# Seven-product MLP, first product: sums formed in seeded PSUM banks, and some deferred steps deferred further

## The chip, the cores and the metric

The kernel runs on one core of one Trainium2 chip. A core has TensorE (PE, matrix products; a weight load, PEld, precedes each and overlaps the one before), VectorE (DVE), ScalarE (ACT), GpSimd (POOL) and SyncE (SP, which issues most transfers). Each engine works off its own instructions in order and waits on semaphores for the others. The metric is the time of one execution on the device in microseconds (us); lower is better.

## The reference, cut to what matters

One encoder layer for 2048 tokens of width 1024: a mixer (attention in two head groups), then an MLP. The change lies in the MLP, mostly in its first product `h @ w1`.

```python
x = x + gt1 * (mixed @ w_o[l])
h = rmsnorm(x, g_norm2[l]) * (1.0 + sc2) + sh2
x = x + gt2 * (jnp.square(jax.nn.relu(h @ w1[l])) @ w2[l])
```

`w1` is 1024 x 4096, `w2` 4096 x 1024, all float32.

## The kernel before

**Tiling.** Everything is stored transposed: features on the partitions, tokens along the row. After the mixer and its output projection (class `Mixed`, eight steps), the MLP is one list `steps` that a loop at the end of the program walks through. The tokens are cut in two halves, `mb` = 1 and then 0, each half into two blocks of 512.

**Seven products.** A 2 x 2 block product is made with seven block products in place of eight (Strassen in Winograd's form). In class `First`, a group `j` (16 per half) is 256 rows of hidden units: two row blocks by two token blocks, contracted over 1024 features in two halves. Sums of the weights' four blocks come from POOL (`sums`, four operations, tiles `ts` and `w`); the sums of the activations' blocks were made ahead (`right_blocks`, tiles `h`). Each of the seven products, named 1 to 7 here as in the code, is one step: four contraction blocks, and for each three matmuls (`mm3`), because every float32 operand is split into a high and a low float32r part. So a step is 12 matmuls of 128 x 512, a group is 84, a half is 1344. Operands are prepared seven or eight steps ahead: ACT casts the high part and DVE subtracts to get the low part (tile `opw`).

**How the products are summed before.** They run in the order 1, 6, 5, 7, 2, 3, 4. Products 1, 6, 5, 7 and 3 each open a bank of PSUM; 2 goes on in the bank of 1, and 4 in that of 7. The other sums are made by DVE on the way out of PSUM: with u = 1 + 6 and v = u + 5, the four results are c11 = 1 + 2, c12 = v + 3, c22 = v + 7 and c21 = u + (7 + 4). ACT copies 1 into SBUF (tile `cu`); DVE adds 6 to it (`cu`), 5 (`cv`), 7 (`cx`), 3 (`cv`) and 4 (`cu`). ACT then applies ReLU and the square to each result (`hidden`, in SBUF; for c11, tile `cy`, straight from PSUM). DVE makes three differences and one more (`ca`, `cb`, `cv`, `ce`) that the second MLP product needs, and SP stores the seven tiles (`keep`, to `scr_hid`).

**Other work in the same steps.** In half 1, `second_sums` (DVE, tile `w2s`) and in half 0 `outer_sums` (DVE, tile `wt`) form sums of `w2` blocks, at the third to sixth step of nearly every group, and SP stores them. `norm2` gets the norm of a token block: ACT squares and DVE sums eight tiles, then `second` sends the sum through PE (`pvm`), POOL and DVE (`ndgm`), and `third` spreads it with PE (`psr`). The second MLP product follows in classes `Second` and `Outer`; `Outer` already works in the order 1, 5, 6, 3, 7, 2, 4 with seeded banks (`ps_s`), and `update` adds results to rows of x and stores them.

**What sets the order.** Program order is the order of the loop: at each step the operands of a later step are prepared, then jobs registered for this step run (`at`), then the step's matmuls and what follows them (`run`), then `later.tick()`, which runs whatever `later.add(n, ...)` put off by n ticks. The loads of `w1` (`load`, tile `w`) stand in SP's queue at the second step of the group two before the one that uses them, behind all the stores of the group before. Banks come from eight buffers in three groups (`zb` four, `ab` two, `db` two); an object of `Banks` hands them out in rotation, `pp` from all three.

Of the kernel before, what the change touches and what calls it, by code (L numbers as in the profile page):

```python
# [9 lines left out]
F32 = mybir.dt.float32  # L10
# [3 lines left out]
ALU = mybir.AluOpType  # L14
# [4 lines left out]
P = 128  # L19
# [60 lines left out]
def encoder_kernel(ctx, tc, xT, c, g1, g2, w_in, w_rest, gqk, bias, w_o, w1, w2, w_ada, b_ada, out):  # L80
# [1199 lines left out]

    NP = DFF // P // 2
    HK = KT // 2
    PRODUCTS = (1, 6, 5, 7, 2, 3, 4)
    PLAIN = (1, 6, 5, 7)
    OUTER = (1, 5, 6, 3, 7, 2, 4)
    HOME = {1: 1, 2: 1, 5: 5, 3: 5, 6: 6, 7: 6, 4: 6}
# [7 lines left out]
    if True:  # L1294
# [4 lines left out]
        hop = {k: pm.enter_context(tc.tile_pool(name=f"hop{k}", bufs=1, side="right")) for k in range(2)}  # L1299
        np2 = pm.enter_context(tc.tile_pool(name="np2", bufs=2, side="right"))  # L1300
        pp = Banks(zb, zb, ab, db, zb, zb, ab, db)

        def operand(src, nm, eng=None, dst=None):

# [18 lines left out]
        def kept(nm):  # L1323
            return accp.tile([P, TB], F32, tag="c", name=f"c{nm}")

        def bank(nm):
            return pp.tile([P, TB], F32, tag="ps", name=f"ps{nm}")

        steps, jobs = [], {}

# [6 lines left out]
        def norm2(tb, step):  # L1337

            acc = rp.tile([P, TB], F32, tag="r", name=f"r{tb}")
            xs = {}  # L1340

            def load(k):
                xs[k] = temp(f"xn{tb}_{k}")
                sp.dma_start(xs[k], scr_x[tb, k])

            def add(k):
                x = xs.pop(k)
                act.activation(x if k else acc, x, AF.Square)
                if k:
                    dve.tensor_tensor(acc, acc, x, op=ALU.add)  # L1350

            def second():
                dg = norm_rstd(np2, pp, acc, f"m{tb}")

                def third():
                    pr = bank(f"r{tb}")
                    for i in range(4):
                        pe.matmul(pr[:, i * P : (i + 1) * P], ones, dg[:, i, :], start=True, stop=True)
                    dve.tensor_copy(acc, pr)
                    rows[tb] = acc  # L1360

                later.add(3, third)

            for k in range(KT):
                at(step + 3 * k, lambda k=k: load(k))
                at(step + 3 * k + 4, lambda k=k: add(k))
            at(step + 3 * KT + 4, lambda: later.add(2, second))

        def right_blocks(mb, k, home):

# [60 lines left out]
        class First(Step):  # L1431
# [3 lines left out]

            def __init__(self, mb, j, i):
                self.mb, self.j, self.i, self.nm = mb, j, i, f"{mb}_{j}_{i}"
                if mb and j == 0 and i in PRODUCTS[:2]:
                    self.tiles = self.frees = 0

            def prepare(self, home=None):
# [32 lines left out]

            def run(self):
                d, i, nm = First.pair[self.mb, self.j], self.i, self.nm
                home = {2: 1, 4: 7}.get(i, i)
                if home == i:
                    d["ps", i] = bank(nm)
                ps = d["ps", home]  # L1480
                for k in range(HK):
                    ks = slice(k * P, (k + 1) * P)
                    h = hops[i, k]
                    first, last = home == i and k == 0, k == HK - 1
                    mm3(ps, self.w[:, 0, ks], self.w[:, 1, ks], h[:, 0, :], h[:, 1, :], first, last, home != i)
                if i == 1:
                    d["u"] = kept(f"u{nm}")
                    act.copy(d["u"], ps)
                if i == 6:
                    column_sum(dve, d["u"], ps, d["u"], ALU.add)  # L1490
                if i == 5:
                    d["v"] = column_sum(dve, kept(f"v{nm}"), ps, d["u"], ALU.add)
                if i == 7:
                    d["c22"] = self.hidden(column_sum(dve, kept(f"x{nm}"), ps, d["v"], ALU.add), 3)
                if i == 2:
                    d["c11"] = kept(f"y{nm}")
                    act.activation(d["c11"], ps, AF.Relu)
                    act.activation(d["c11"], d["c11"], AF.Square)
                    c11 = d["c11"]
                    later.add(2, lambda: self.keep(1, c11))  # L1500
                if i == 3:
                    c12 = self.hidden(column_sum(dve, d["v"], ps, d["v"], ALU.add))

                    def rest():
                        t1 = column_sum(dve, kept(f"a{nm}"), c12, d["c11"], ALU.subtract)
                        self.keep(5, t1)
                        d["t2"] = column_sum(dve, kept(f"b{nm}"), d["c22"], t1, ALU.subtract)
                        self.keep(6, d["t2"])
                        self.keep(7, column_sum(dve, c12, d["c22"], c12, ALU.subtract))

                    later.add(2, rest)
                if i == 4:
                    c21 = self.hidden(column_sum(dve, d["u"], ps, d["u"], ALU.add), 2)

                    def end():
                        self.keep(4, column_sum(dve, kept(f"e{nm}"), c21, d["t2"], ALU.subtract))
                        del First.pair[self.mb, self.j]

                    later.add(2, end)

            def hidden(self, c, i=None):
                act.activation(c, c, AF.Relu)
                act.activation(c, c, AF.Square)
                if i:
                    later.add(2, lambda: self.keep(i, c))
                return c
# [88 lines left out]
        def update(mb, r, odd, acc, loads, adds, keep=True):  # L1615

            d = Second.whole

            def fetch(n):
                d["x", r, 1 - odd, n] = x = (temp if keep else kept)(f"xu{mb}_{r}{odd}_{n}")  # L1620
                sp.dma_start(x, scr_x[2 * mb + odd, HK * r + n])

            def add(n):
                x = d["x", r, 1 - odd, n]
                weigh(x, d[acc, n], HK * r + n)
                if keep:
                    later.add(1, lambda: sp.dma_start(scr_x[2 * mb + odd, HK * r + n], x))

            for n in range(HK):
                at(loads[n], lambda n=n: fetch(n))  # L1630
                at(adds[n], lambda n=n: add(n))

        def plain(mb, i):

            f = len(steps)
            steps.extend(Second(mb, i, j) for j in range(NP))
            spread = lambda *ns: [f + n for n in ns]
            if i == 6:
                update(mb, 0, 1, "s", spread(0, 1, 2, 6), spread(4, 5, 6, 10))
            if i == 5:  # L1640
                update(mb, 0, 0, "v", spread(11, 12, 13, 14), spread(16, 17, 18, 19))
            if i == 7:
                update(mb, 1, 0, "v", spread(4, 5, 6, 7), spread(9, 10, 11, 12), False)
                update(mb, 1, 1, "s", spread(10, 11, 12, 13), spread(16, 17, 18, 19))
            return f
# [27 lines left out]
        class Outer(Step):  # L1673
# [33 lines left out]
            def run(self):  # L1707
                pr, k = self.pr, self.k
                home = HOME[pr]
                for n in range(2):  # L1710
                    if k == 0 and pr in (1, 5):
                        Outer.banks[pr, n] = bank(f"{self.nm}_{n}")
                    ps = Outer.banks[home, n]
                    ns = slice(n * P, (n + 1) * P)
                    begun = pr not in (1, 5)
                    mm3(
                        ps, self.l[:, 0, k % 2, ns], self.l[:, 1, k % 2, ns], self.r[:, 0, :], self.r[:, 1, :],
                        k == 0 and not begun, k == HP - 1, begun,
                    )
                if k == HP - 1:  # L1720
                    for n in range(2):
                        self.end(n)

            def end(self, n):
                pr, ps = self.pr, Outer.banks[HOME[self.pr], n]
                if pr == 1:
                    Outer.banks[6, n] = bank(f"{self.nm}_s{n}")
                    act.copy(Outer.banks[6, n], ps)
                for b, last in {5: (("22", 0),), 6: (("12", 0),), 3: (("12", 1),), 7: (("22", 1),), 2: (("11", 1),), 4: (("21", 1),)}.get(pr, ()):
                    x = Outer.outs[b, n]  # L1730
                    mb, row, odd = self.place(b, n)
# [238 lines left out]
```

## Time and profile before

| | |
|---|---|
| median of 3 runs | 2582.88 us (2582.31 to 2586.53) |
| profiled execution | 2583.59 us, of which its span 2581.9 us |
| granted TensorE clock, mean | 0.999 |
| DVE instructions | 3401 |
| ACT instructions | 2785 |

In the profile, a row such as `ps<-h,opw` names the tile written, an arrow and the tiles read. The number after the form is how many instructions were merged into the row, and the brackets give how long the engine was idle before it and which instruction ended that wait. MATMUL durations overlap: one takes about 0.39 us, but the next starts about 0.23 us after it. The first MLP product of half 1 takes place between 1365 and 1686 us of the span, its second product until 1867, the first product of half 0 until 2174, and the rest until the end.

### The profile page before, as it was taken

Reading aid. Unit: us, or ns where it says so; the run is one execution under the profiler, and the core shown is the slowest. Engines: PE = TensorE matmul, PEld = TensorE weight load, DVE = VectorE, ACT = ScalarE, POOL = GpSimd, SP = SyncE. Lnnn points to the kernel's source line nnn. Section 1 sums busy time; section 2 is a strip of 40 time slices with the busy share of each in tenths; the row PEclk is TensorE's granted clock in tenths of the full one; section 3 lists DMA queues with packets and bytes.
Section 4 is the critical chain, followed back from the end, with each engine's and each line's share of the span. In section 5 each row is a group of like instructions: output and inputs, shape, how many; then the busy total and the mean of one; then the engine's idle time right before and its main releaser. Section 6 shows DMA issues by size and latency. Waiting matters only on the chain. (4 is left out here: it accounts for less than half of the span.)

```text
span 2581.9 us, 39420 instructions
## 1 busy us (share of the span) xinstructions
PE 2546.8 (99%) x12484; PEld 2112.9 (82%) x12484; DVE 2031.6 (79%) x3401; ACT 1448.3 (56%) x2785; POOL 950.4 (37%) x1256
## 2 busy tenths in 40 slices
PE   9999999999999999999999999999999999999999
PEld 7888888888888888887888877887888878888887
DVE  7656767887789879998768787777787886798987
ACT  6333435668866676666744544565444445465655
POOL 4330144777766677677603333200123320000000
PEclk9999999999999999999999999999999999999999
DMA  9879879788887788756787876786577766866773
GB/s 354 330 296 363 336 286 290 215 238 277 272 262 233 234 281 260 240 195 195 226 331 245 290 261 247 261 302 236 212 248 266 250 241 241 315 222 242 266 272 123
DMA packets 276944, 674.80 MB, mean 261 GB/s; under 512 B 29952, under 2 KB 75008, under 8 KB 266112
## 3 DMA queue, kind: packets, MB, share of 16 engines
q1 hardware_dynamic: 275440, 667.57, 74.7%
q10 hardware_dynamic: 1296, 4.72, 0.4%
q8 instruction: 99, 1.62, 0.3%
q14 instruction: 109, 0.89, 0.1%
HBM read 461.93 MB, written 210.24 MB: 260 GB/s over the span
## 5 line engine op out<-in xcount | busy, mean ns | idle before, releaser
L42 PE MATMUL ps<-h,opw 128*128 128x512 f32 x2664 | 609.9, 390 | 4.0 <-ACT cu L42 2.4
L42 PEld LDWEIGHTS ps<-h,opw 128*128 128x128 f32 x2664 | 498.1, 188 | 113.8 <-ACT cu L42 5.7
L42 PE MATMUL ps<-oph,opv 128*128 128x512 f32 x1536 | 353.3, 391 | 2.7 <-ACT opv L42 1.6
L42 POOL TENSOR_TENSOR b<-p 128x512 f32<-128x512 f32 (+1 forms) x320 | 292.5, 914 | 168.1 <-DVE p L42 92.1
L42 ACT CAST wth<-wt 128x512 fp32r<-128x512 f32 (+3 forms) x544 | 257.7, 484 | 172.3 <-PE wt L42 162.3
L42 PEld LDWEIGHTS ps<-oph,opv 128*128 128x128 f32 x1536 | 289.0, 188 | 66.3 <-ACT opv L42 2.7
L42 DVE TENSOR_TENSOR wtl<-wt,wth 128x512 fp32r<-128x512 f32 (+3 forms) x544 | 291.7, 548 | 59.4 <-ACT wth L42 56.9
L42 PE MATMUL pt<-w,ht 128*128 128x512 f32 x1248 | 288.2, 391 | 0.0
L42 POOL TENSOR_TENSOR ts<-w 128x512 f32<-128x512 f32 x32 | 48.5, 1515 | 616.9 <-DMA w<-in_w_dram 516.0
L42 PEld LDWEIGHTS pt<-w,ht 128*128 128x128 f32 x1248 | 233.0, 188 | 47.7
L42 DVE TENSOR_TENSOR_SCAN p<-z,p,zero 128x512 f32<-128x512 f32 x192 | 245.9, 1282 | 25.7 <-ACT z L42 18.3
L42 PE MATMUL acc<-wth,v 128*128 128x512 f32 (+3 forms) x544 | 220.6, 410 | 0.0
L42 ACT ACTIVATE z<-z 128x512 f32<-128x512 f32 (+1 forms) x320 | 166.5, 521 | 55.1 <-PE z L42 49.3
L42 PE MATMUL z<-k,q 128*128 128x512 f32 (+3 forms) x640 | 185.6, 371 | 7.8 <-DVE p L42 7.1
L42 DVE TENSOR_TENSOR opw<-w,opw 128x512 fp32r<-128x512 f32 x127 | 100.8, 796 | 111.5 <-ACT opw L42 111.5
L42 PE MATMUL acc<-wtl,v 128*128 128x512 f32 (+3 forms) x544 | 185.4, 347 | 0.0
L42 POOL TENSOR_TENSOR e<-e,cols 128x640 f32<-128x640 f32 (+4 forms) x128 | 142.9, 1123 | 83.3 <-DVE cols L42 57.1
L42 PE MATMUL wt<-ident,b 128*128 128x128 f32 x1088 | 171.4, 273 | 1.0 <-DVE cols L42 0.3
L42 PEld LDWEIGHTS wt<-ident,b 128*128 128x128 f32 x1088 | 136.3, 140 | 42.2 <-DVE wtl L42 1.9
L42 PE MATMUL po<-fx,ow 128*128 128x512 f32 x576 | 161.7, 393 | 1.0 <-DMA ow<-scr_wo 1.0
L42 DVE TENSOR_TENSOR oph<-hw,oph 128x512 fp32r<-128x512 f32 x128 | 90.4, 706 | 80.0 <-ACT oph L42 80.0
L42 ACT CAST opr<-r 128x512 fp32r<-128x512 f32 x168 | 104.7, 625 | 83.2 <-PE ps L42 46.6
(210 smaller groups left out, 4849.2 us busy)
## 6 DMA issues: line engine op xcount, KB each, us to landing
q<-scr_q SPq DMA_DIRECT2D x128, 256.0 KB, 5.2
w<-in_w_dram SPq DMA_DIRECT2D x64, 512.0 KB, 5.5
hw<-scr_hid SPq DMA_DIRECT2D x64, 512.0 KB, 6.3
k<-scr_k SPq DMA_DIRECT2D x240, 128.0 KB, 4.4
v<-scr_v SPq DMA_DIRECT2D x120, 256.0 KB, 4.1
wa<-in_w_ada_dram SPq DMA_DIRECT2D x48, 512.0 KB, 6.2
ow<-scr_wo SPq DMA_DIRECT2D x24, 1024.0 KB, 5.9
hw<-scr_s SPq DMA_DIRECT2D x48, 512.0 KB, 7.0
```

The lines of the kernel that those rows point to most:

```text
L42: return lambda *x, **y: self.tc.keep_in_program_order(f(*x, **y))
```

## The change

`First` takes the order and the bank scheme of `Outer`. Products 1 and 5 open banks of a new rotation `fresh`; after product 1, ACT copies the bank into a bank of the rotation `seeded` (the two buffers `ab`), and products 6, 7 and 4 go on there; 3 goes on in the bank of 5, and 2 in that of 1. After products 5 and 6 ACT copies their banks to SBUF (tile `cp`). DVE then needs two additions in place of five: c12 = copy of (1 + 6) + bank (5 + 3) after product 3, and c22 = copy of 5 + bank (1 + 6 + 7) after product 7. c11 and c21 stand complete in their banks, and ReLU reads them there. `Outer` and the norm take their banks from the two new rotations too; `Second` and `Mixed` stay with `pp`.

Apart from that, the deferrals get longer: `second` of the norm 2 to 3 ticks, `third` 3 to 6, the stores in `update` 1 to 3, and one load and one addition in `update` move two steps back.

```diff
-    PRODUCTS = (1, 6, 5, 7, 2, 3, 4)
...
+        fresh, seeded = Banks(zb, zb, db), Banks(ab)
...
-                dg = norm_rstd(np2, pp, acc, f"m{tb}")
+                dg = norm_rstd(np2, fresh, acc, f"m{tb}")
...
-                    pr = bank(f"r{tb}")
+                    pr = bank(f"r{tb}", fresh)
...
-                later.add(3, third)
+                later.add(6, third)
...
-            at(step + 3 * KT + 4, lambda: later.add(2, second))
+            at(step + 3 * KT + 4, lambda: later.add(3, second))
...
-                home = {2: 1, 4: 7}.get(i, i)
-                if home == i:
-                    d["ps", i] = bank(nm)
-                ps = d["ps", home]
+                home = HOME[i]
+                if i in (1, 5):
+                    d["ps", i] = bank(nm, fresh)
+                ps, begun = d["ps", home], i not in (1, 5)
...
                 if i == 1:
-                    d["u"] = kept(f"u{nm}")
-                    act.copy(d["u"], ps)
-                if i == 6:
-                    column_sum(dve, d["u"], ps, d["u"], ALU.add)
-                if i == 5:
-                    d["v"] = column_sum(dve, kept(f"v{nm}"), ps, d["u"], ALU.add)
+                    d["ps", 6] = bank(f"{nm}_s", seeded)
+                    act.copy(d["ps", 6], ps)
+                if i in (5, 6):
+                    d["p", i] = kept(f"p{nm}")
+                    act.copy(d["p", i], ps)
+                if i == 3:
+                    d["c12"] = self.hidden(column_sum(dve, d["p", 6], ps, d["p", 6], ALU.add))
                 if i == 7:
-                    d["c22"] = self.hidden(column_sum(dve, kept(f"x{nm}"), ps, d["v"], ALU.add), 3)
+                    d["c22"] = self.hidden(column_sum(dve, d["p", 5], ps, d["p", 5], ALU.add), 3)
                 if i == 2:
-                    d["c11"] = kept(f"y{nm}")
-                    act.activation(d["c11"], ps, AF.Relu)
-                    act.activation(d["c11"], d["c11"], AF.Square)
...
+                    c11 = self.hidden(kept(f"y{nm}"), 1, ps)
...
                 if i == 4:
-                    c21 = self.hidden(column_sum(dve, d["u"], ps, d["u"], ALU.add), 2)
+                    c21 = self.hidden(kept(f"z{nm}"), 2, ps)
...
-            def hidden(self, c, i=None):
-                act.activation(c, c, AF.Relu)
+            def hidden(self, c, i=None, src=None):
+                act.activation(c, c if src is None else src, AF.Relu)
...
-                    later.add(1, lambda: sp.dma_start(scr_x[2 * mb + odd, HK * r + n], x))
+                    later.add(3, lambda: sp.dma_start(scr_x[2 * mb + odd, HK * r + n], x))
...
-                update(mb, 0, 1, "s", spread(0, 1, 2, 6), spread(4, 5, 6, 10))
+                update(mb, 0, 1, "s", spread(0, 1, 2, 8), spread(4, 5, 6, 12))
...
-                        Outer.banks[pr, n] = bank(f"{self.nm}_{n}")
+                        Outer.banks[pr, n] = bank(f"{self.nm}_{n}", fresh)
...
-                    Outer.banks[6, n] = bank(f"{self.nm}_s{n}")
+                    Outer.banks[6, n] = bank(f"{self.nm}_s{n}", seeded)
...
-            steps += [First(mb, j, i) for j in range(NP) for i in PRODUCTS]
+            steps += [First(mb, j, i) for j in range(NP) for i in OUTER]
```

More of the change, by code (lines that the diff above doesn't have):

```diff
@@ L1324, in kept, with bank @@
             return accp.tile([P, TB], F32, tag="c", name=f"c{nm}")
-        def bank(nm):
-            return pp.tile([P, TB], F32, tag="ps", name=f"ps{nm}")
+        def bank(nm, banks=pp):
+            return banks.tile([P, TB], F32, tag="ps", name=f"ps{nm}")
         steps, jobs = [], {}
@@ L1437, in __init__ @@
                 self.mb, self.j, self.i, self.nm = mb, j, i, f"{mb}_{j}_{i}"
-                if mb and j == 0 and i in PRODUCTS[:2]:
+                if mb and j == 0 and i in OUTER[:2]:
                     self.tiles = self.frees = 0
@@ L1483, in run @@
                     h = hops[i, k]
-                    first, last = home == i and k == 0, k == HK - 1
-                    mm3(ps, self.w[:, 0, ks], self.w[:, 1, ks], h[:, 0, :], h[:, 1, :], first, last, home != i)
+                    mm3(
+                        ps, self.w[:, 0, ks], self.w[:, 1, ks], h[:, 0, :], h[:, 1, :],
+                        k == 0 and not begun, k == HK - 1, begun,
+                    )
                 if i == 1:
-                    d["u"] = kept(f"u{nm}")
-                    act.copy(d["u"], ps)
@@ L1493, in run @@
                 if i == 7:
-                    d["c22"] = self.hidden(column_sum(dve, kept(f"x{nm}"), ps, d["v"], ALU.add), 3)
+                    d["c22"] = self.hidden(column_sum(dve, d["p", 5], ps, d["p", 5], ALU.add), 3)
                 if i == 2:
-                    d["c11"] = kept(f"y{nm}")
-                    act.activation(d["c11"], ps, AF.Relu)
-                    act.activation(d["c11"], d["c11"], AF.Square)
-                    c11 = d["c11"]
-                    later.add(2, lambda: self.keep(1, c11))
@@ L1501, in run @@
-                if i == 3:
-                    c12 = self.hidden(column_sum(dve, d["v"], ps, d["v"], ALU.add))
+                    c11 = self.hidden(kept(f"y{nm}"), 1, ps)
                     def rest():
-                        t1 = column_sum(dve, kept(f"a{nm}"), c12, d["c11"], ALU.subtract)
+                        c12, c22 = d["c12"], d["c22"]
+                        t1 = column_sum(dve, kept(f"a{nm}"), c12, c11, ALU.subtract)
                         self.keep(5, t1)
-                        d["t2"] = column_sum(dve, kept(f"b{nm}"), d["c22"], t1, ALU.subtract)
+                        d["t2"] = column_sum(dve, kept(f"b{nm}"), c22, t1, ALU.subtract)
@@ L1508, in rest @@
                         self.keep(6, d["t2"])
-                        self.keep(7, column_sum(dve, c12, d["c22"], c12, ALU.subtract))
+                        self.keep(7, column_sum(dve, c12, c22, c12, ALU.subtract))
                     later.add(2, rest)
                 if i == 4:
-                    c21 = self.hidden(column_sum(dve, d["u"], ps, d["u"], ALU.add), 2)
+                    c21 = self.hidden(kept(f"z{nm}"), 2, ps)
                     def end():
```

## The prediction

> **What bounds the kernel now.** The page first: whole span, PE's line, and the costliest group.
>
> ```profile
> span 2581.9 us, 39420 instructions
> PE 2546.8 (99%) x12484; PEld 2112.9 (82%) x12484; DVE 2031.6 (79%) x3401; ACT 1448.3 (56%) x2785; POOL 950.4 (37%) x1256
> L42 PE MATMUL ps<-h,opw 128*128 128x512 f32 x2664 | 609.9, 390 | 4.0 <-ACT cu L42 2.4
> ```
>
> PE is the bound, and the change neither adds nor removes a matmul. So only PE's gaps can move the time. Their places come from PE's timeline over the MLP.
>
> ```profile
> 1365.86 5.60 PE L42 MATMUL ps<-h,opr 128*128 128x512 f32 x24
> ```
> ```profile
> 1472.30 5.78 PE L42 MATMUL ps<-h,opw 128*128 128x512 f32 x24 [0.20 <-ACT cu L42]
> 1478.56 13.89 PE L42 MATMUL ps<-h,opw 128*128 128x512 f32 x60 [0.48 <-DVE cx L42]
> ...
> 1498.51 0.95 PE L42 MATMUL pvm<-ones,r 128*128 128x1 f32 x8
> 1499.32 8.46 PE L42 MATMUL ps<-h,opw 128*128 128x512 f32 x36
> 1510.56 1.13 PE L42 MATMUL psr<-ndgm,ones 128*128 128x128 f32 x8 [2.78 <-DVE ndgm L42]
> 1511.44 43.83 PE L42 MATMUL ps<-h,opw 128*128 128x512 f32 x192
> ...
> 1599.66 1.16 PE L42 MATMUL psr<-ndgm,ones 128*128 128x128 f32 x8 [2.17 <-DVE ndgm L42]
> ...
> 1685.93 66.33 PE L42 MATMUL ps<-oph,opv 128*128 128x512 f32 x289
> ...
> 1867.20 201.74 PE L42 MATMUL ps<-h,opw 128*128 128x512 f32 x888
> ...
> 2174.11 87.20 PE L42 MATMUL ps<-oph,opv 128*128 128x512 f32 x384
> ...
> 2282.91 11.04 PE L42 MATMUL ps_s<-opr,ol 128*128 128x512 f32 x48
> 2293.79 11.04 PE L42 MATMUL ps<-opr,ol 128*128 128x512 f32 x48
> ```
>
> The last two rows give the pace without a gap: 10.88 us for 48 matmuls, 0.2267 each, so a step of 12 is 2.72 us and a half of 1344 is 304.64 us. Half 1 took 1685.93 - 1365.86 = 320.07. Its norm matmuls need about 0.81 + 0.88 per norm (from the starts around 1498.51 and 1510.56), 3.4 for two. So 320.07 - 304.64 - 3.4 = 12.0 us are lost there, 2.78 + 2.17 = 4.95 of it in front of the norm's spreading and 7.1 in short waits for `cu` (the ACT copy that frees the bank of product 1) and `cx` (the addition that frees the bank of product 7). Half 0 took 2174.11 - 1867.20 = 306.91 and loses 2.3.
>
> **The change part by part.**
>
> *The old waits.* They come from DVE and ACT running behind. DVE's five additions on the way out of PSUM become two per group, at these prices:
>
> ```profile
> L42 DVE TENSOR_TENSOR cu<-ps,cu x64: 676/684/692, 1378.7 to 2174.3; 128x512 f32<-128x512 f32 x64
> L42 ACT COPY cu<-ps x32: 565/577/590, 1374.9 to 2158.0; 128x512 f32<-128x512 f32 x32
> ...
> L42 ACT COPY ps_s<-ps x6: 570/570/571, 2271.5 to 2512.1; 128x512 f32<-128x512 f32 x6
> ```
>
> That is 32 x 3 x 0.684 = 66 us less work on DVE, and 32 x 2 x 0.577 = 37 us more on ACT (the seeding at 0.57 replaces the old copy). Neither is PE time by itself. With two us less per group of 19.04 us (7 x 2.72), DVE should no longer fall behind, so I take the old short waits as gone: -7.1 and -2.3.
>
> *The norm.* `third` comes six steps after `second`, 16.3 us, in place of three. The `psr` row came 12.05 us after the `pvm` row, so its operand is there in time: -4.95. The price of the norm's own matmuls stays. If DVE and POOL needed 16 us, some of it would come back; the bound is 0 to -4.95, and I take the whole.
>
> *The ACT copies.* The seed is needed one product after it can start, as are the copies of 5 and 6: 2.72 us for 0.57 to 0.58. What stands ahead of them on ACT is a cast of 0.61 or at most a ReLU pair of 1.30 and a cast, 1.9. So they hide; without that cover each microsecond late costs one on PE.
>
> *The addition c22.* Here the change adds a wait. Product 4 used to go on in the bank of 7, with products 2 and 3 between; now only product 2 lies between, and 4 must wait until DVE has read the bank of 7. The queue in front of that addition on DVE is: c12's addition (after product 3), the low part of an operand whose high part ACT makes only after c12's ReLU and square, then one `wt` or `w2s` sum, then c22's addition. The same chain stands in the trace of before, in half 0, with `cx` in the role of c12 and `opw`, `wt` behind it:
>
> ```profile
> 1895.43 0.69 DVE L42 TENSOR_TENSOR opw<-w,opw 128x512 fp32r<-128x512 f32 x1
> ...
> 1896.03 0.69 DVE L42 TENSOR_TENSOR wt<-wt 128x512 f32<-128x512 f32 x1
> ...
> 1897.32 0.69 DVE L42 TENSOR_TENSOR cx<-ps,cv 128x512 f32<-128x512 f32 x1 [0.60 <-PE ps L42]
> 1898.05 1.30 ACT L42 ACTIVATE cx<-cx 128x512 f32<-128x512 f32 x2 [2.78 <-DVE cx L42]
> 1899.25 0.61 ACT L42 CAST opw<-w 128x512 fp32r<-128x512 f32 x1
> 1899.63 1.29 POOL L42 TENSOR_TENSOR ts<-w 128x512 f32<-128x512 f32 x1 [11.66 <-DMA w<-in_w_dram]
> 1899.89 1.59 DVE L42 TENSOR_TENSOR opw<-w,opw 128x512 fp32r<-128x512 f32 x1 [1.88 <-ACT opw L42]
> ...
> 1901.01 1.63 POOL L42 TENSOR_TENSOR ts<-ts,w 128x512 f32<-128x512 f32 x1
> ...
> 1901.40 1.79 DVE L42 TENSOR_TENSOR wt<-wt 128x512 f32<-128x512 f32 x1
> 1902.60 1.73 POOL L42 TENSOR_TENSOR w<-w 128x512 f32<-128x512 f32 x1
> 1903.11 1.77 DVE L42 TENSOR_TENSOR opw<-ts,opw 128x512 fp32r<-128x512 f32 x1
> ...
> 1904.30 1.74 POOL L42 TENSOR_TENSOR ts<-w,ts 128x512 f32<-128x512 f32 x1
> ...
> 1912.85 0.69 DVE L42 TENSOR_TENSOR ce<-cu,cb 128x512 f32<-128x512 f32 x1
> ...
> 1913.97 0.91 SPq L42 DMA_DIRECT2D w<-in_w_dram  x2
> ...
> 1919.91 1.29 POOL L42 TENSOR_TENSOR ts<-w 128x512 f32<-128x512 f32 x1 [13.88 <-DMA w<-in_w_dram]
> ```
>
> Between the end of product 3 and the earliest start of 4 lie two products less the overlap of a matmul, 2 x 2.72 - (0.39 - 0.23) = 5.28 us. Undisturbed, the chain is 2.57 (1897.32 to 1899.89), two operations at 0.60 from start to start (1895.43 to 1896.03), and 0.69: 4.46, and it hides with 0.8 to spare. But here, with POOL at work, the two operations took 1.59 and 1.79, and the next one started at 1903.11, 5.79 after the first. With 0.69 behind it c22 would be ready at 6.48: PE would stand for 1.2 us. Each DVE operation with both inputs in SBUF ended 0.55 us after the POOL operation it ran into (1901.48 to 1900.92, 1903.19 to 1902.64), while additions that read PSUM never took over 0.692 (row above). So the price is bounded: if the first operation only just meets the end of one of POOL's, 2.57 + 0.60 + 1.70 + 0.69 = 5.56, a stall of 0.3; if it waits out a whole one of 1.74 and 0.55 more, 2.57 + 2.25 + 1.70 + 0.69 = 7.2, a stall of 1.9. I take 1.1, the middle, which is near the 1.2 of that row.
>
> The Trainium skill ("SBUF — State Buffer", "Who interferes with whom") says the same of the cause: a VectorE operation with two SBUF inputs is locked out until a GpSimd operation that reads SBUF has ended, it does not share bandwidth. Were it a half-and-half share instead, each of the two would take 1.2, and the stall would be 0.4 a group, 10 us in all; the rows above bear out the lock.
>
> *Does POOL run just then?* POOL's four sums take 1.29 + 1.63 + 1.73 + 1.74 = 6.4 us once per group, and start when the load of `w` has landed. SP issues that load right behind the store of `ce`; from the end of `ce` (1913.54) to POOL's start is 6.37. In the changed kernel `ce` ends about 4.5 us after a group's first matmul. This is an estimate: c22 ends 2.8 before the group does; DVE then waits 1.9 for ACT as after any result, does `opw` and a sum (1.2); ACT's next pair and cast (1.8 after its last cast) hold the next `opw` until 3.6 after c22; and that, three differences, an `opw` and `ce`, six at 0.6, end 7.3 after c22. So POOL would start at 4.5 + 6.4 = 10.9 and run to 17.3; product 3 ends near 11.0, the two operations start at 13.6 and later. Both are hit whenever POOL starts between about 8.6 and 13.6. In the rows above `cx` starts as the fourth product ends, 4 x 2.72 + 0.16 = 11.04 after the group's first matmul, so POOL started 13.35 after it, with the `ce` before it held up by a DVE that was behind.
>
> The stall needs both POOL's sums and a `wt` or `w2s` sum in place: groups 1 to 13 of half 1 and 1 to 12 of half 0, 25 in all: 25 x 1.1 = +27.5. In two groups of half 1 a norm addition stands in the same place too, one more at 1.7: +3.4.
>
> *Outer and Second.* `Second` takes a bank of `ab` for its third row block, and after two of the three `Outer` runs this is the bank that product 4 just left. DVE read it late:
>
> ```profile
> 2337.37 3.79 PE L42 MATMUL ps<-oph,opv 128*128 128x512 f32 x16
> ...
> 2339.09 1.41 DVE L42 SCALAR_TENSOR_TENSOR txo<-ps_s,mod,txo 128x512 f32<-128x512 f32 x2 [0.90 <-DMA txo<-scr_x]
> ```
>
> The third block starts six matmuls in, 2337.37 + 1.36 = 2338.73; half of the 1.41 is done at 2339.80. So 1.1 us, twice: +2.2 (bounds 0, if the row of x lands earlier, to 2.8, both operations).
>
> *The stores of `update`.* They go behind two more steps of SP's loads. In half 1's second product these rows wait for DVE as the loads around them do, so I take 0, bounds -3 to +3.
>
> **Sum.** 2583.59 - 4.95 - 7.1 - 2.3 + 27.5 + 3.4 + 2.2 = 2602.3. The profiled execution stood 0.7 above the median, so 2602 as a median (2601.6 rounded up).
>
> **The rivals.**
>
> *No collision, faster.* POOL starts after about 14.2 us in the group, or before 7, and c22 hides with its 0.8. Then 2583.59 - 14.35 + 2.2 = 2571.4, or 2571 as a median. For it: POOL started at 13.35 above, not far off. Against it: that start was late because `ce` was, and `ce` comes earlier once DVE keeps up.
>
> *Half a collision, about the same.* POOL starts between 13.6 and 14.2, only the second operation is hit, and the stall is 0 to 0.5: 2571.4 + 25 x 0.3 = 2579, or 2578 as a median.
>
> *DVE stays behind, much slower.* If the additions saved do not bring DVE up to PE, product 4 pays the lag of c22 in each group, since it has 2.72 of cover where it had 5.44. With a lag of 4.5 as just before the wait at 1478.56 (PE waits only when the lag and 0.69 exceed 5.28), that is 4.5 + 0.69 - 2.56 = 2.6 in some 20 groups, 52 us: 2583.6 - 4.95 + 52 = 2631. It decides from a lag of 1.9. Against it: 66 us of work less.
>
> *The clock falls.* Short stalls might lower the granted clock. One did:
>
> ```profile
> 1771.08 5.17 PE L42 MATMUL ps<-oph,opv 128*128 128x512 f32 x13 [1.59 <-ACT opv L42]
> ```
> ```profile
> 1771.00:1776.00 5.00, 4.84 (x13) 3.67 (x14) 5.00 (x9) 1.69 (x4) 0.00 (x0) 0.66 0.97 359
> ```
>
> After 1.59 us idle the clock was 0.66 over five microseconds, 1.7 lost. At 25 stalls that is +42, 2645. Against it: the longer waits of 2.78 and 2.17 were followed at full pace. The Trainium skill ("TensorE: Matmul & The Clock Gate", "Why this matters for your kernels") puts the limit at idle gaps over some 3 us, by which none of these would count; the row of 1.59 contradicts that as a sharp limit.
>
> **How the numbers follow.** Forecast 0.60; no collision 0.18; half a collision 0.12; DVE behind 0.07; clock 0.03. The forecast's own range goes with the stall: 25 x 0.3 to 25 x 1.9 in place of 27.5 gives 2582 to 2622 as medians. For eight in ten I go from 2571, the point of the faster rival, to 2616, which leaves out the two dear rivals and the upper end of my own. About 0.2%, 5 us, is what a measurement of this kernel tells from no change. Faster than 2577.7: 0.18 and a third of the half collision, 0.22. Between: the rest of it and the lower end of my own, 0.14. Slower: 0.64.
>
> **What would show it.** Before the matmuls of product 4, a wait on the DVE addition `cp` of about 1 us in some 25 groups, with POOL's `ts` rows over the `opw` and `wt` or `w2s` ahead of it; no wait before `psr`; none of note on ACT's copies into `ps_s` and `cp`; 1 us at the third block of two `Second` runs. I am wrong if POOL's first sum starts past 14 us of a group, if DVE's additions are late by more than the collision, or if the copies on ACT hold PE.

## The result, and the profile after

| | before | after |
|---|---|---|
| median of 4 runs | 2583.18 us (2582.31 to 2586.53) | 2608.68 us (2606.53 to 2618.36) |
| ratio, 95% interval | | 1.0104 (1.0077 to 1.0130) |
| profiled execution | 2583.59 us, span 2581.9 | 2606.53 us, span 2604.8 |

The changed kernel is about 1% slower, 25.5 us in the medians and 22.9 us between the two profiled spans. The page of the changed kernel: its first part and the group of the seeded products:

```profile
span 2604.8 us, 39355 instructions
PE 2550.7 (98%) x12484; PEld 2113.8 (81%) x12484; DVE 1950.0 (75%) x3305; ACT 1481.3 (57%) x2849; POOL 933.4 (36%) x1256
...
L42 PE MATMUL ps_s<-h,opw 128*128 128x512 f32 x1152 | 281.8, 394 | 26.9 <-DVE cp L42 23.6
```

DVE is busy for 82 us less, with 96 instructions fewer, and still PE waits 23.6 us for it ahead of the seeded products alone. PE's timeline after (start, duration, and in brackets the idle time before the row and what ended it) shows where:

```profile
1375.27 4.49 PE L42 MATMUL ps_s<-h,opw 128*128 128x512 f32 x12 [3.33 <-ACT ps_s L42]
...
1449.62 3.01 PE L42 MATMUL ps_s<-h,opw 128*128 128x512 f32 x12 [2.64 <-DVE cp L42]
...
1530.72 1.06 PE L42 MATMUL psr<-ndgm,ones 128*128 128x128 f32 x8
...
1572.29 3.03 PE L42 MATMUL ps_s<-h,opw 128*128 128x512 f32 x12 [1.89 <-DVE cp L42]
...
1619.69 1.06 PE L42 MATMUL psr<-ndgm,ones 128*128 128x128 f32 x8
...
1909.99 3.01 PE L42 MATMUL ps_s<-h,opw 128*128 128x512 f32 x12 [0.99 <-DVE cp L42]
...
2183.75 3.01 PE L42 MATMUL ps<-h,opw 128*128 128x512 f32 x12 [1.73 <-ACT cp L42]
...
2360.42 42.47 PE L42 MATMUL ps<-oph,opv 128*128 128x512 f32 x186 [0.94 <-DVE txo L42]
2481.20 42.50 PE L42 MATMUL ps<-oph,opv 128*128 128x512 f32 x186 [0.75 <-DVE txo L42]
```

In 24 of the 32 groups PE waits for c22's addition (`cp`), once each and 0.98 us in the mean (0.21 to 2.64): 12.6 us in half 1 and 11.0 in half 0. A wait costs more than its idle time: the 0.39 - 0.23 by which matmuls otherwise overlap, and 12 matmuls that take 3.01 in place of 2.88, together 0.29. So the 24 waits cost 23.6 + 24 x 0.29 = 30.6 us. The first row is another wait, of ACT's seed copy, once, and the row at 2183.75 one of ACT's copy of product 5, once.

One of the 24 groups, DVE and POOL of the changed kernel with PE's two products:

```profile
1902.96 1.51 POOL L42 TENSOR_TENSOR ts<-w 128x512 f32<-128x512 f32 x1 [11.68 <-DMA w<-in_w_dram]
...
1903.60 0.69 DVE L42 TENSOR_TENSOR cp<-ps,cp 128x512 f32<-128x512 f32 x1 [0.29 <-PE ps L42]
...
1905.80 1.29 POOL L42 TENSOR_TENSOR w<-w 128x512 f32<-128x512 f32 x1
1906.12 2.88 PE L42 MATMUL ps<-h,opw 128*128 128x512 f32 x12
1906.16 1.47 DVE L42 TENSOR_TENSOR opw<-w,opw 128x512 fp32r<-128x512 f32 x1 [1.88 <-ACT opw L42]
1907.05 1.74 POOL L42 TENSOR_TENSOR ts<-w,ts 128x512 f32<-128x512 f32 x1
1907.56 1.77 DVE L42 TENSOR_TENSOR wt<-wt 128x512 f32<-128x512 f32 x1
1909.26 0.68 DVE L42 TENSOR_TENSOR cp<-ps_s,cp 128x512 f32<-128x512 f32 x1
```

c12's addition starts at 1903.60 as product 3 ends, without delay. The operand's low part then takes 1.47 in place of 0.69 and ends 0.54 after POOL's third sum (1907.63 to 1907.09); the `wt` sum takes 1.77 and ends 0.54 after the fourth (1909.33 to 1908.79). c22 is ready at 1909.94, 6.34 after the chain began, and PE starts product 4 at 1909.99.

### The profile page after: what moved, and what is told of

It reads as the page before. It is cut to its first block, busy times and chain, and to the rows that moved or that the text cites. A ratio compares the mean times of both kernels' runs of the same rounds, so it can differ in the third digit from the quotient of the medians.

```text
span 2604.8 us, 39355 instructions
## 1 busy us (share of the span) xinstructions
PE 2550.7 (98%) x12484; PEld 2113.8 (81%) x12484; DVE 1950.0 (75%) x3305; ACT 1481.3 (57%) x2849; POOL 933.4 (36%) x1256
## 4 chain that ended last, share of the span: by engine, by line
PE 73%; DVE 11%; DMA 5%; ACT 5%; issue 4%; POOL 1%; SPq 1%; DVEq 0%; POOLq 0%; ACTq 0%
PE ps L42 22%; PE pt L42 11%; PE ps_s L42 9%; PE acc L42 6%; PE wt L42 6%; PE po L42 4%; PE pf L42 4%; PE z L42 4%; PE pq L42 3%; PE cz L42 2%; PE pso L42 2%; DVE p L42 2%; DVE cp L42 1%; DVE opr L42 1%; DVE w2s L42 1%
## 5 line engine op out<-in xcount | busy, mean ns | idle before, releaser
L42 PE MATMUL ps<-h,opw 128*128 128x512 f32 x1512 | 358.9, 389 | 1.7 <-ACT cp L42 1.7
L42 PEld LDWEIGHTS ps<-h,opw 128*128 128x128 f32 x1512 | 283.9, 188 | 61.2 <-ACT cp L42 2.2
L42 PE MATMUL ps_s<-h,opw 128*128 128x512 f32 x1152 | 281.8, 394 | 26.9 <-DVE cp L42 23.6
L42 PEld LDWEIGHTS ps_s<-h,opw 128*128 128x128 f32 x1152 | 215.0, 188 | 81.5 <-DVE cp L42 33.7
L42 DVE TENSOR_TENSOR opw<-w,opw 128x512 fp32r<-128x512 f32 x127 | 111.4, 880 | 125.6 <-ACT opw L42 125.6
L42 ACT ACTIVATE cp<-cp 128x512 f32<-128x512 f32 x128 | 80.9, 632 | 181.2 <-DVE cp L42 179.1
```

The costliest lines, as they stand in the source:

```text
L42: return lambda *x, **y: self.tc.keep_in_program_order(f(*x, **y))
```

## The experiments

Times are medians. The last column is the time that PE stood idle ahead of product 4 for DVE's addition that frees its bank (`cp` in the new order, `cx` in the old), between 1360 and 2200 us, from the groups by line in that stretch; in the kernel before it was 1.6.

| kernel | us | ratio to before, 95% interval | idle ahead of 4 |
|---|---|---|---|
| after | 2608.7 | 1.0104 (1.0077 to 1.0130) | 23.6 |
| e7, no sums on POOL | 2573.5 | 0.9952 (0.9938 to 0.9965) | 0.0 |
| e2, sum out of the chain | 2581.0 | 0.9983 (0.9974 to 0.9992) | 2.0 |
| e1, load later | 2590.0 | 1.0015 (1.0006 to 1.0024) | 9.3 |
| e1b, load earlier | 2615.4 | 1.0116 (1.0103 to 1.0130) | 24.8 |
| e4, before with load later | 2622.1 | 1.0144 (1.0130 to 1.0158) | 29.0 |
| e6, seed first | 2605.1 | 1.0071 (1.0056 to 1.0087) | 26.0 |
| e3, deferrals alone | 2582.3 | 0.9988 (0.9979 to 0.9996) | 6.1 |
| e5, no deferrals | 2610.7 | 1.0094 (1.0080 to 1.0107) | 21.9 |
| e8, combined | 2574.6 | 0.9955 (0.9942 to 0.9967) | 2.1 |
| e9, rows of x earlier | 2575.9 | 0.9965 (0.9952 to 0.9979) | 2.0 |
| e10, before with the same sums | 2577.2 | 0.9969 (0.9957 to 0.9982) | 5.2 |

The theory under test (A): POOL's four sums run into the DVE operations ahead of c22. Against it stood that DVE is behind by its own work (B), that ACT's new copies hold PE (C), and that the deferrals did it (D).

**e7, POOL's sums left out.** The operands of products 5, 6, 7 and 3 are plain blocks of w1, so these four sums are missing from what is computed.

```diff
-                s1, s2, s4 = (temp(f"s{self.nm}_{n}") for n in (0, 1, 3))
-                s3 = d["21"]
-                column_sum(pool, s1, d["21"], d["22"], ALU.add)
-                column_sum(pool, s2, s1, d["11"], ALU.subtract)
-                column_sum(pool, s3, d["11"], d["21"], ALU.subtract)
-                column_sum(pool, s4, d["12"], s2, ALU.subtract)
+                s1, s2, s3, s4 = d["21"], d["22"], d["11"], d["12"]
```

> The changed kernel without POOL's four sums in the first product: the operands of products 5, 6, 7 and 3 are the plain blocks of w1, so the result is not that of the reference. DVE, ACT, PE and SP keep every instruction. Theory A: the low part and the sum ahead of c22 take 0.69 each, the chain 4.46 us, the waits before product 4 vanish but for the two norm groups, and the late seeding of the first group goes too: 2608.7 - 28 - 5 = 2576 (2570 to 2582). Rival B (DVE behind by its own work) and C (ACT's copies): waits of 20 us or more stay, 2600 to 2610.

DVE's and PE's rows at the same place of e7's timeline:

```profile
1881.99 0.69 DVE L42 TENSOR_TENSOR cp<-ps,cp 128x512 f32<-128x512 f32 x1 [0.28 <-PE ps L42]
...
1884.55 0.69 DVE L42 TENSOR_TENSOR opw<-w,opw 128x512 fp32r<-128x512 f32 x1 [1.87 <-ACT opw L42]
1885.16 0.69 DVE L42 TENSOR_TENSOR wt<-wt 128x512 f32<-128x512 f32 x1
1885.76 0.69 DVE L42 TENSOR_TENSOR cp<-ps_s,cp 128x512 f32<-128x512 f32 x1
...
1887.23 2.88 PE L42 MATMUL ps_s<-h,opw 128*128 128x512 f32 x12
```

With the same instructions on DVE and ACT the chain takes 1886.45 - 1881.99 = 4.46 us, product 4 starts 5.24 after c12's addition, and no wait is left ahead of it in either half. B and C fall for these waits. The two norm groups came free too, which was not expected. This kernel has less to do than the reference asks, so it is not a version to use. The wait for the first group's seed is gone in it too, and its time shows about what curing both can bring.

**e2, a sum taken out of the chain.** POOL stays where it is.

```diff
-                at(step + n + (0 if j else 4), lambda x=x: out(*x))
+                at(step + n + n // 2 + (0 if j else 4), lambda x=x: out(*x))
...
-                at(step + n, lambda x=x: sums(*x))
+                at(step + n + n // 2, lambda x=x: sums(*x))
```

> The changed kernel with the third and fourth sum of w2 blocks (w2s in half 1, wt in half 0) one step later each, so that only the low part of an operand stands between c12's and c22's addition on DVE. POOL is left where it is. Theory A: the chain is 2.57 + up to 1.6 + 0.69 = 4.9 us, under the 5.28 of cover, so the waits before product 4 fall from 28.8 to under 8, all but the two groups with a norm addition, and the time to about 2587 (2583 to 2593). Rival B (DVE behind): an operation of 0.6 is out of the way in 25 groups, at most 15 us, 2594 to 2600. Rival C (ACT): no change, 2605 to 2612.

2581.0, six us below the forecast of theory A and two below its range, and 2.0 us of idle time are left of 23.6. In e2's timeline POOL still collides with the operand's low part:

```profile
1968.32 0.69 DVE L42 TENSOR_TENSOR cp<-ps,cp 128x512 f32<-128x512 f32 x1 [0.29 <-PE ps L42]
...
1970.47 1.30 POOL L42 TENSOR_TENSOR ts<-ts,w 128x512 f32<-128x512 f32 x1
...
1970.88 1.43 DVE L42 TENSOR_TENSOR opw<-w,opw 128x512 fp32r<-128x512 f32 x1 [1.87 <-ACT opw L42]
...
1972.24 0.68 DVE L42 TENSOR_TENSOR cp<-ps_s,cp 128x512 f32<-128x512 f32 x1
```

The 1.43 is there, but the chain is 4.60 us long, within the 5.28 of cover, and costs nothing. B allowed at most 15 us and was too small for the 27.7 gained.

**e1 and e1b, the load of w1 moved.** SP's load decides when POOL starts.

```diff
-                    at(begin + max(7 * j - 13, 2 if mb else -6), f.load)
+                    at(begin + max(7 * j - 11, 2 if mb else -6), f.load)
```

> The changed kernel with the load of w1 two steps later in SP's order (fourth step of a group in place of the second), nothing else. Theory A (POOL's four sums run into the two DVE operations ahead of c22's addition): POOL's first sum starts at about 15 us of a group in place of 10.4 to 10.9, the low part and the sum ahead of c22 go back to about 0.69 each, the waits before product 4 fall from 28.8 us in all to under 6, and the time from 2608.7 to about 2585 (2580 to 2590). Rival B (DVE is simply behind, because c22 has one product of cover less): DVE has the same work, so the waits stay at 25 us or more and the time at 2605 to 2612. Rival C (the copies on ACT hold PE): the same as B. If A is right the late first step of half 1 (4.5 us idle before product 6 of the first group) stays, since the first groups load at the same place.

With the later load all waits ahead of product 4 in half 0 are gone. POOL's sums start not at 15 us of a group, as expected, but at the head of the next one (in one group they run from 1.7 to 8.1 us). They meet the differences there, and DVE has caught up by c12's addition, which is late by 0.9 us at most in groups 1 to 13. In half 1 eight waits of 0.85 to 1.74 stay, where c12's addition is late itself; why DVE does not catch up there was not followed further. So the time fell by 19 of the 24 us expected.

e1b has `7 * j - 15` in that place.

> The changed kernel with the load of w1 two steps earlier in SP's order (last step of the group ahead), so that it stands in front of the store of ce and not behind it. Theory A: if POOL's first sum then starts before 7 us of a group, all four are over when the two DVE operations start at 13.6, the waits before product 4 go as with the later load, and the time is about 2584 (2578 to 2590); if it starts between 8.6 and 13.6, they stay and the time is 2605 to 2610. Rivals B and C: the place of the sums does not matter, 2605 to 2612 in either case.

POOL's first sum started at 7.2 to 8.1 us of a group in nearly all of half 0, between the two cases of the expectation, and the time is no better than that of the changed kernel. The timeline of e1b:

```profile
1987.46 1.28 POOL L42 TENSOR_TENSOR ts<-w 128x512 f32<-128x512 f32 x1 [13.47 <-DMA w<-in_w_dram]
1987.50 1.79 DVE L42 TENSOR_TENSOR wt<-wt 128x512 f32<-128x512 f32 x1
...
1992.62 0.68 DVE L42 TENSOR_TENSOR cp<-ps,cp 128x512 f32<-128x512 f32 x1
...
1996.38 0.68 DVE L42 TENSOR_TENSOR cp<-ps_s,cp 128x512 f32<-128x512 f32 x1
1997.12 2.12 PE L42 MATMUL ps_s<-h,opw 128*128 128x512 f32 x8 [0.52 <-DVE cp L42]
```

The chain from c12 to c22 is undisturbed (1992.62 to 1997.06, 4.44), yet PE waits: now POOL stretches three operations ahead of c12's addition (the first is shown), which starts without a bracket, late, where it had waited 0.29 for PE. So theory A was too narrow in one point: not only the two operations behind c12 count, but every DVE operation from which no idle time separates c22.

**e4, the control: the kernel before with the load later.** The same edit as e1.

> Control: the kernel before with the load of w1 two steps later, the edit that moved the changed kernel from 2608.7 to 2590. Theory A (the place of POOL's sums matters because the change left c22's addition one product of cover in place of two): here the cover is still two products, so the time moves by less than 5 us: 2580 to 2589. If the later load is a gain by itself, whatever the order of the products: 2565 to 2572.

Both expectations are wrong: 2622.1, 37 us slower. DVE and POOL in one group of e4:

```profile
2016.73 1.75 POOL L42 TENSOR_TENSOR ts<-w 128x512 f32<-128x512 f32 x1 [14.68 <-DMA w<-in_w_dram]
2017.25 1.78 DVE L42 TENSOR_TENSOR cv<-cx,cv 128x512 f32<-128x512 f32 x1
...
2020.65 1.78 DVE L42 TENSOR_TENSOR ce<-cu,cb 128x512 f32<-128x512 f32 x1
...
2022.35 1.77 DVE L42 TENSOR_TENSOR opw<-ts,opw 128x512 fp32r<-128x512 f32 x1
...
2027.65 0.68 DVE L42 TENSOR_TENSOR cx<-ps,cv 128x512 f32<-128x512 f32 x1
2028.39 4.84 PE L42 MATMUL ps<-h,opw 128*128 128x512 f32 x20 [1.58 <-DVE cx L42]
```

Four operations in a row are stretched to about 1.77 (three are shown), six more follow without a gap, then `cx`, and PE waits for it. With five additions per group DVE has no room to catch up at this place, and two products of cover are not enough. The waits before `psr` grew too, from 4.9 to 10.7 us. In the kernel before, unedited, the sums ran just after `cx`:

```profile
1957.34 0.69 DVE L42 TENSOR_TENSOR cx<-ps,cv 128x512 f32<-128x512 f32 x1
...
1960.15 1.60 POOL L42 TENSOR_TENSOR ts<-w 128x512 f32<-128x512 f32 x1 [12.72 <-DMA w<-in_w_dram]
1960.52 1.79 DVE L42 TENSOR_TENSOR wt<-wt 128x512 f32<-128x512 f32 x1
...
1968.17 0.69 DVE L42 TENSOR_TENSOR opw<-w,opw 128x512 fp32r<-128x512 f32 x1 [1.88 <-ACT opw L42]
```

Three operations are stretched, then DVE has a pause (the 1.88), and the next `cx` is a whole group away. So the price lies not in how much is stretched, but in where. Groups by line over twelve groups of half 0 show it, first before (1886 to 2115 us), then after (1892 to 2136):

```profile
L42 DVE TENSOR_TENSOR wt<-wt 128x512 f32<-128x512 f32 x46 | 54.5, 1186 | 0.0
L42 DVE TENSOR_TENSOR opw<-w,opw 128x512 fp32r<-128x512 f32 x47 | 36.6, 779 | 43.2 <-ACT opw L42 43.2
L42 DVE TENSOR_TENSOR opw<-ts,opw 128x512 fp32r<-128x512 f32 x35 | 34.9, 996 | 0.4 <-ACT opw L42 0.4
```

```profile
L42 DVE TENSOR_TENSOR wt<-wt 128x512 f32<-128x512 f32 x48 | 46.0, 958 | 0.0
L42 DVE TENSOR_TENSOR opw<-w,opw 128x512 fp32r<-128x512 f32 x48 | 41.6, 868 | 50.0 <-ACT opw L42 50.0
L42 DVE TENSOR_TENSOR opw<-ts,opw 128x512 fp32r<-128x512 f32 x36 | 24.8, 690 | 37.9 <-ACT opw L42 37.9
```

Over the 0.69 of an undisturbed operation, the kernel before lost 46 x 0.50 + 47 x 0.09 + 35 x 0.31 = 38 us of DVE's time to POOL in these rows, at next to no cost (all of its half 0 loses 2.3 us). The changed kernel lost only 48 x 0.27 + 48 x 0.18 = 22, and yet PE stood idle for 11.0 us.

**e6, the first group's seed.** Operands two and five ahead at the first two steps of half 1, and POOL's last two sums exchanged.

```diff
                 column_sum(pool, s2, s1, d["11"], ALU.subtract)
+                column_sum(pool, s4, d["12"], s2, ALU.subtract)
                 column_sum(pool, s3, d["11"], d["21"], ALU.subtract)
-                column_sum(pool, s4, d["12"], s2, ALU.subtract)
...
-            while nxt is not None and ready - used + nxt.tiles <= 8:
+            room = {KT: 2, KT + 1: 5}.get(n, 8)
+            while nxt is not None and ready - used + nxt.tiles <= room:
```

> The changed kernel with the operands of the first two steps of half 1 limited (two ahead at the first step, five at the second, eight from then on) and POOL's third and fourth sum exchanged, so that ACT's copy that seeds the first group is not behind casts that wait for POOL. Nothing else moves in the groups after but the order of the two sums. If the 3.33 us before the seeded product of the first group, and the slow 12 matmuls after it (4.49 us in place of 2.9), come from those casts, both go: 5 us, 2601 to 2606. If the copy is late for another reason: 2607 to 2612. The waits before product 4 should stay at about 28 us by theory A, since POOL starts where it did.

The seed's wait is gone, and 0.93 for a copy `cp` is left one product later. In e7, without POOL's sums, it is gone too. So the casts that waited for POOL are the cause, as supposed. The median is 3.6 us less, but the interval of its ratio overlaps that of the changed kernel, so the gain in time is not settled. In the changed kernel ACT's rows before that wait read:

```profile
1370.61 0.62 ACT L42 CAST opw<-ts 128x512 fp32r<-128x512 f32 x1 [2.77 <-POOL ts L42]
...
1374.00 0.62 ACT L42 CAST opw<-ts 128x512 fp32r<-128x512 f32 x1 [0.17 <-POOL ts L42]
1374.64 0.57 ACT L42 COPY ps_s<-ps 128x512 f32<-128x512 f32 x1
```

Seven casts stand between, two of them held by POOL; the seed copy follows at 1374.64, while product 5 had ended near 1372.

**e3 and e5, the deferrals.** e3 is the kernel before with the deferral lines of the diff alone, e5 the changed kernel without them.

> The kernel before with the deferrals of the change alone (second of the norm after 3 ticks, third after 6, stores of update after 3, the one load and addition of update two steps later); order and banks of the first product as before. My step of the prediction: the two waits before psr go (4.95 us), the stores move nothing, so 2578 (2576 to 2580). Rival D (the deferrals cost what the change lost): 2590 or more.

> The changed kernel with the old deferrals (second 2 ticks, third 3, stores of update 1, load and addition as before); order, seeding and banks of the change stay. My theory (the deferrals only help, by the waits before psr): up to 4.95 us slower than the changed kernel, 2609 to 2615, with waits before both psr rows. Rival D (the deferrals are what made the change slow): 2590 or less.

e3 stands at 2582.3 beside a kernel before of 2585.1 in the same series, by the ratio a gain of 3.1 us (1.0 to 5.4). The gain is not the 4.95 of the norm, though. In its profile the waits before `psr` are gone, but those for `cu` and `cx` in half 1 grew from 3.3 to 9.6, two of them (1.25 and 2.20) close to the norms, and the first product of half 1 took 324.1 us in place of 320.1. What got shorter is half 1's second product, 177.2 in place of 181.3. e5 is not told apart from the changed kernel (2610.7 and 2608.7, overlapping intervals), and its `psr` rows have no wait either, against the expectation. But in half 1's second product it waits for ACT's `opv` as the kernel before did (1.59 at 1771.08):

```profile
1782.93 6.09 PE L42 MATMUL ps<-oph,opv 128*128 128x512 f32 x24 [1.27 <-ACT opv L42]
```

That stretch took 180.6 us in e5. It took 181.3 in the kernel before and in e4, the other two without the longer deferrals, and 177.0 to 179.6 in all ten that have them. So the deferrals in `update` shorten it. D falls: the deferrals did not make the change slow. The waits before `psr` end by either cause, the longer deferral or a DVE with less to do; but in the old order the deferral only moved the time to other waits.

**e8, e9 and e10, towards a better version.** e8 is e2 and e6 together, with this:

```diff
-        pp = Banks(zb, zb, ab, db, zb, zb, ab, db)
+        pp = Banks(zb, zb, db, ab, zb, zb, db, ab)
```

> The changed kernel with three edits: the third and fourth sums of w2 blocks one step later (as in e2), the seeding of the first group ahead of the casts (as in e6), and the banks of Second in the order zb, zb, db, ab, so that its fourth and not its third row block meets the bank that Outer's product 4 left. From e2's 2581.0: -5 for the first group, -1.5 for the two Second runs: 2574 to 2577, faster than both kernels. If the edits get in each other's way (the sums move POOL or ACT in the first group): 2580 or more.

2574.6, as expected, but the bank order had no part in it: PE still waited 1.36 and 0.81 us, now at the fourth row block, because DVE's `txo` operations waited for their row of x. e9 leaves `pp` as it was and moves that load:

```diff
-                at(f + HP * OUTER.index(pr) + 1, lambda s=s, b=b: s.load_x(b))
+                at(f + HP * OUTER.index(pr) + (1 if pr != 4 else -2), lambda s=s, b=b: s.load_x(b))
```

> The changed kernel with the sums of w2 blocks moved (as in e2) and the seeding first (as in e6), Second's banks as in the change, and the rows of x that Outer's product 4 is added to loaded three steps earlier. In e8, with the other order of banks, PE still waited 1.36 and 0.81 us at the fourth row block, and DVE's additions there had waited 1.95 us for the row of x. If that load is what holds the bank, both waits go: 2571 to 2574. If the bank itself was the matter (DVE late for other reasons): e8's time or 2 us more, 2574 to 2578.

In e9's profile both waits are gone and the span is 2568.8, against e8's 2572.6; but its five times spread from 2570.5 to 2577.2, and the median lies where the other case was expected. So the load is what held the bank, and what it is worth in the median is not settled. Last, e10 puts e2's moved sums and the deferrals on the kernel before:

> The kernel before with the deferrals of the change and the third and fourth sums of w2 blocks one step later: what the edits that cure the changed kernel are worth without the new order and the seeded banks. If the cured order is itself worth something (its 66 us less of DVE's work end the short waits of half 1, 7.1 us): this one stays behind e8 and e9, at 2578 to 2584, with short waits for cu and cx in half 1. If the moved sums alone do it: 2572 to 2577.

2577.2 lies between the two expectations, and its profile keeps waits of 0.23 to 2.11 for `cu` and `cx` in half 1. A part of its gain is that of the deferrals alone (e3). The rest, some 5 us by the ratios, is that of the moved sums, but the intervals of e3 and e10 just overlap, so that the sums help the old order too is likely and not shown. The profiles of e8 and e10 show what the cured new order gives and takes: half 1's first product took 314.1 us in place of 321.1, that of half 0 307.0 in place of 304.6, and the rest after it 410.4 in place of 407.8. So the 7 us of short waits in half 1 are won, and some 5 of them are lost again to the copy in the last group and to `Second` after `Outer`. Whether e8 beats e10 in the median is left open by their intervals. Both are faster than the kernel before and the changed one.

## Why the prediction came out as it did

The forecast was 2602 (2571 to 2616), slower; measured 2608.7, slower and within the range. The collision, its main step, came as forecast; three smaller steps were wrong. Point by point:

- **The collision.** Mechanism and place as forecast. In half 0 `ce` ended 4.46 after a group's first matmul (forecast 4.5), POOL started at 10.4 to 11.3 (10.9), and the chain took 6.34 in the group above (6.48). In half 1 `ce` ended at 4.5 to 6.7 and POOL started at 10.4 to 14.1, so that some groups paid only half a collision (a wait of 0.21) and others more than the forecast. The two groups with a norm addition in the chain are the rows of 2.64 and 1.89. Group 7 of half 1, one of the 25, has no wait; there the norm's spreading stands ahead of product 4 (1530.72). In all 25 x 1.1 + 3.4 = 30.9 was forecast and 30.6 measured. That the two are so close is in part luck: 14.5 against 13.2 in half 0, 16.1 against 17.7 in half 1.
- **The old waits and `psr`.** All 14.35 us came back. But for `psr` the deferral was named as the reason, and this step is not borne out: the waits are gone without it (e5), and the deferral alone brought half 1's first product nothing (e3). A DVE with less to do is the reason that is left.
- **Second after Outer.** Forecast +2.2; 0.94 and 0.75 idle, and the rest of the kernel after half 0 longer by 2.25 in all. The bank was named, and DVE reading it late; e8 and e9 show that DVE's own wait, for the row of x, is what lasts.
- **The ACT copies: a step that failed.** "So they hide" was argued from a steady group, and holds there (e7). At the two ends of the product it does not. In the first group the seed's 3.33, its 0.16 of lost overlap, and 4.49 for 12 matmuls in place of 2.88 (the granted clock was 0.72 between 1374 and 1380) make 5.1 us. In the last one ACT's copy of product 5 stood behind a cast that waited 4.81 us for a tile of the second product (`hw`), which gave the 1.73 at 2183.75, 2.0 with the 0.29. The prediction knew the cast ahead of a copy, but not what that cast itself waits for.
- **The stores of `update`: a term put at nothing.** Its bounds were -3 to +3, but half 1's second product was 3.9 us shorter (177.34 in place of 181.27), of which 3.3 are the wait of 1.59 at 1771 of before and the 1.7 of clock behind it, which did not come again. By e3 and e5 above this is the doing of the deferrals in `update`; whether of the stores or of the one load and addition is not separated.

The sum with the measured terms: -14.35 + 30.6 + 2.25 + 5.1 + 2.0 - 3.9 + 0.5 (a later start of the first product, 1366.34 against 1365.86) = +22.2, of the 22.9 between the spans. The median stood 2.2 above the profiled execution, the fastest of the four; most of the rest of the 6.7 between forecast and median is the copies, 7.1, less the second product, 3.9. These two errors were of opposite sign, so the forecast came this close in part by luck.

The rival "no collision" priced the kernel at 2571: e7 shows what that price was worth, 2573.5 with POOL's sums out of the way. The rival "the clock falls" priced 25 drops: behind none of the 24 waits did 12 matmuls take over 3.03 us, and only the 3.33 of the first group brought a drop. The rival "DVE stays behind" is wrong for the changed kernel but is what e4 does to the kernel before.

## What to carry to other kernels

When an order of work shortens the time between an operation and its deadline, follow the whole queue ahead of that operation, and count each element at the price it has when the other engine is running, not at its mean. The same collisions can be free or cost 1% of the time, depending on whether idle time lies between them and the next deadline. And cost a copy that "hides" at the first and the last turn of a loop too, where the work ahead of it on its engine waits for something else.

## What was not expected of the hardware

The clock after a wait. Two waits of equal length in e1b, and PE's rows behind them:

```profile
1467.81 3.01 PE L42 MATMUL ps_s<-h,opw 128*128 128x512 f32 x12 [2.48 <-DVE cp L42]
...
1592.07 4.61 PE L42 MATMUL ps_s<-h,opw 128*128 128x512 f32 x12 [2.48 <-DVE cp L42]
...
1896.55 4.61 PE L42 MATMUL ps_s<-h,opw 128*128 128x512 f32 x12 [2.03 <-DVE cp L42]
```

The windows of e1b around them (length, busy time of five engines, then PE's granted clock, the DMA share and GB/s):

```profile
1466.00:1472.00 6.00, 4.20 (x18) 3.49 (x19) 3.75 (x7) 4.15 (x8) 0.00 (x0) 1.00 0.26 102
1591.00:1597.00 6.00, 4.93 (x15) 3.90 (x16) 3.72 (x7) 3.69 (x7) 0.00 (x0) 0.72 0.28 107
...
1895.00:1901.00 6.00, 4.45 (x13) 3.51 (x14) 2.96 (x5) 3.57 (x7) 0.00 (x0) 0.72 0.44 114
```

After one wait of 2.48 us the clock stayed at 1.00, after the other, and after one of 2.03, it was 0.72 over six us and 12 matmuls took 1.6 us longer; after 2.64 in the changed kernel (1449.62 above) they took 3.01. So the length of one wait does not decide. The Trainium skill ("TensorE: Matmul & The Clock Gate", "Part 1: The HAM clock gate") describes a monitor that halves the clock after an idle window of about 3.4 us, a window that runs freely. If a wait can begin anywhere in such a window, it would fit that equal waits end differently, but the waits of 2.03 here and 1.59 before are shorter than a whole window, and no run tests it.
